# Layer B's sample result: turned in the bank `o` of the value product instead of the bank `tp` of the transposed queries and keys

## The chip, the cores and the metric

The kernel runs on one core of one Trainium2 chip. The metric is device time in microseconds (us) of one execution; lower is better. Engines are named as in the profile: PE is TensorE's matmul, PEld its weight load, DVE is VectorE, ACT is ScalarE, POOL is GpSimd, SP is the engine whose queue issues the DMAs.

## The reference, cut to what matters

Two layers of gated attention over a prompt of 2048 tokens and a "sample" of 64 new tokens with a cache. The second layer (B) has 16 heads of 64, a band of the own chunk of 64 and 8 chunks before it, and a bias by clipped distance:

```
q, k, v, gate = split(rms_norm(x) @ w_in)        # q and k normed per head
s = q @ k.T / 8 + bias(q_pos - k_pos)            # band for the prompt, cache + own for the sample
o = softmax(s) @ v
y = x + (o * silu(gate)) @ w_out
```

The sample goes through the same formula with 256 cached keys and its own 64.

## The kernel before

**Tiling.** Layer B goes through its 16 heads in eight passes of two heads each (`hp` = 0 to 7). In each pass the prompt is cut into units of 256 tokens (two tiles of 128), and the 64 sample tokens are a unit of their own. The order in a pass is prompt units 0 to 6, then the sample, then prompt unit 7. All products are float32 data in two float32r parts (a high and a low one).

**Order.** TensorE's order is written out by hand. Between the small steps of attention (scores, transposes of the weights, value products) a "filler" puts matmuls of the next input projection (lines 477 to 479, PSUM tile `pj`), and in the last pass those of the output projection (lines 1366 to 1368). The other engines' order is left to the tile scheduler, which follows its own estimate of times; semaphores between the engines come from the tiles that instructions share.

**Steps for a prompt unit.** `queries` (line 1072) transposes normed queries and keys into the PSUM tile `tp` (four transposes `tp<-ident,pa`); ACT takes the high parts out of it (lines 1095 and 1096), DVE the low parts (line 1100 for queries, line 1104 for keys, into `KA` and `KB`). The low parts are queued as background work. `scores` writes tile `sb` (lines 1146 and 1147); DVE adds the bias and takes the extreme (line 1150); ACT does the exponential (line 1154). `values` transposes the weights into `sb` (five `sb<-ident,p`), ACT and DVE split them into `ph` and `pl` (lines 581 and 582). `outputs` multiplies with the values into tile `o` (lines 1242 and 1243). On the second head it also transposes the gate tile `G` into `tp`. `G` is made on POOL (line 1168) out of reciprocals that DVE takes at line 1160.

**Steps for the sample.** `sample_outputs` multiplies weights and values into `o` (lines 1205 and 1206), ACT and DVE add the halves into an SBUF tile `o1` (lines 1209 and 1211), POOL multiplies with the gate (line 1212). Some steps later `sample_turned` (line 1214) transposes this tile once, and ACT writes the two halves out of PSUM, with the factor 0.5, into another `o1` tile (line 1219), which SP stores (line 1220).

**PSUM.** `tp` and `o` are tiles of one bank with one buffer each (`psum("tp", 512, 1)`, `psum("o", 512, 1)`), `pj` has two buffers, and `sb` has two of two banks each. A new tile in a pool of one buffer waits until every reader of the tile before it has finished.

**Place of the sample's steps.** While unit 7 is at work, the steps come in this order on PE: `values` of the sample, `values` of unit 7's first tile with `sample_outputs`, then `queries` of the next pass's unit 0 (which takes `tp`), a `scores`, another `values`, and then `sample_turned`. So in passes 0 to 6 the last tile in `tp` before the sample's transpose is that of the next pass's queries and keys. In pass 7 there is no next pass.

Of the kernel before, what the change touches and what calls it, by code (L numbers as in the profile page):

```python
# [50 lines left out]
def hybrid_encoder_kernel(  # L51
# [43 lines left out]
    def t(tag, shape, bufs=2, dt=F32):  # L95
        uid[0] += 1
        return sb.tile(shape, dt, tag=tag, name=f"{tag}_{uid[0]}", bufs=bufs)

    def psum(tag, cols, bufs, pool=None):
        uid[0] += 1  # L100
        return (pool or pp).tile([P, cols], F32, tag=tag, name=f"{tag}_{uid[0]}", bufs=bufs)
# [505 lines left out]
    def transpose(out, in_):  # L607
        n = in_.shape[0]
        nc.tensor.transpose(out, in_, ident[:n, :n])  # L609
# [396 lines left out]
    def layer_b():  # L1006
# [187 lines left out]
        def then(it, i, h):  # L1194
            if it.unit[0] == NU:
                return [lambda: sample_outputs(it), lambda: sample_turned(it)]
            if i == len(it.unit[2]) - 1:
                return [lambda: outputs(it, h)]
            return []
# [12 lines left out]
            nc.gpsimd.tensor_tensor(o, it.G[:, 0:HD], o, op=ALU.mult)  # L1212

        def sample_turned(it):
            tp = psum("tp", 512, 1)
            transpose(tp[0:HD, 0:P], it.o)
            o = t("o1", [P, 256])[:, 0:TS]
            for hh, r in enumerate(halves):
                nc.scalar.activation(o[r], tp[0:HD, hh * TS : (hh + 1) * TS], AF.Identity, scale=0.5)
            store(og[1][:, it.hp, SEQ:TOK], o)  # L1220
            finished[1, NU] = finished.get((1, NU), 0) + 1
# [290 lines left out]
```

## Time and profile before

| | us |
|---|---|
| median of 3 runs | 2322.2 (2320.93 to 2326.36) |
| the profiled execution, its time | 2330.51 |
| its span, first to last instruction | 2328.7 |
| PE busy | 2259.3 |
| DVE, ACT, POOL busy | 1559.2, 1432.8, 839.5 |
| mean granted TensorE clock, share of full speed | 0.991 |

All starts below are us from the start of the profiled span. A row of the timeline reads: start, duration, engine, line, operation, output tile <- input tiles, shapes, count, and in brackets the idle time of this engine just before, with the instruction that ended it. Layer B's attention runs from about 880 to 2170; what stands before is layer A, and behind it the rest of the output projection.

### The profile page before, as it was taken

The page shows a single profiled execution, that of the slowest core. Times are in us where ns is not written, and L with a number is a line of the kernel's source. Part 1 is how long each engine was busy: PE and PEld are TensorE (multiplying, and loading weights), DVE is VectorE, ACT ScalarE, POOL GpSimd, SP SyncE. Part 2 cuts the span into 40 slices and gives each one's busy share as a digit, 9 for nine tenths or more (in the row PEclk, how much of TensorE's full clock was granted, in tenths as well). Part 3 has the DMA queues.
Part 4 walks back from the last instruction along what each step waited for, and adds up shares of the span by engine and source line. Part 5 has one row for each costly group of instructions (what it writes and reads, how often), then busy time and mean ns, then how long its engine had stood idle before and what let it go on. Part 6 is the DMA issues. An engine that isn't in the chain of part 4 may idle for free.

```text
span 2328.7 us, 42202 instructions
## 1 busy us (share of the span) xinstructions
PE 2259.3 (97%) x13869; PEld 1984.3 (85%) x13869; DVE 1559.2 (67%) x5194; ACT 1432.8 (62%) x3632; POOL 839.5 (36%) x1196
## 2 busy tenths in 40 slices
PE   7899999999999999999999999999999999999999
PEld 6787888888889998888888888888888888888999
DVE  6779888887784446776767757667667577576211
ACT  6778877777773336765656656656556566565321
POOL 5554533333354556432222222222223222224443
PEclk9999999999999999999999999999999999999999
DMA  8846546754437767454543544544445435443665
GB/s 250 265 152 204 170 147 189 220 176 159 141 110 208 226 212 261 157 184 125 167 126 104 175 133 129 154 134 119 139 134 158 125 113 174 123 125 106 187 186 148
DMA packets 232124, 379.35 MB, mean 163 GB/s; under 512 B 24720, under 2 KB 163360, under 8 KB 231872
## 3 DMA queue, kind: packets, MB, share of 16 engines
q1 hardware_dynamic: 231904, 376.65, 52.7%
q8 instruction: 109, 1.79, 0.3%
q14 instruction: 111, 0.91, 0.1%
HBM read 296.13 MB, written 82.08 MB: 162 GB/s over the span
## 4 chain that ended last, share of the span: by engine, by line
PE 79%; DVE 8%; DMA 5%; ACT 4%; issue 2%; POOL 1%; SPq 1%; DVEq 0%; ACTq 0%; POOLq 0%
PE pj L477 13%; PE pj L479 12%; PE pj L478 12%; PE pj L1366 5%; PE pj L1367 5%; PE pj L1368 5%; PE sb L609 5%; PE o L1243 3%; PE o L1242 3%; PE tp L609 3%; PE sb L1147 3%; PE sb L1146 3%; DMA xraw<-in_x_rows_dram 2%; PE sa L609 2%; DVE pl L582 1%
## 5 line engine op out<-in xcount | busy, mean ns | idle before, releaser
L477 PE MATMUL pj<-wh,xx 128*128 128x512 f32 (+1 forms) x1648 | 671.0, 407 | 9.2 <-ACT pb L500 8.6
L479 PE MATMUL pj<-wh,xx 128*128 128x512 f32 (+1 forms) x1648 | 641.3, 389 | 0.0
L478 PE MATMUL pj<-wl,xx 128*128 128x512 f32 (+1 forms) x1648 | 638.7, 388 | 1.0 <-DVE wl L312 1.0
L479 PEld LDWEIGHTS pj<-wh,xx 128*128 128x128 f32 x1648 | 312.6, 190 | 68.3
L477 PEld LDWEIGHTS pj<-wh,xx 128*128 128x128 f32 x1648 | 314.1, 191 | 50.3 <-ACT pb L500 9.9
L478 PEld LDWEIGHTS pj<-wl,xx 128*128 128x128 f32 x1648 | 314.8, 191 | 40.0 <-DVE wl L312 1.4
L383 POOL TENSOR_TENSOR xx<-xraw,xx 128x528 fp32r<-128x528 f32 (+1 forms) x200 | 264.9, 1341 | 197.1 <-ACT xx L382 185.0
L540 POOL TENSOR_TENSOR f<-f,mhalf 128x4 f32<-128x4 f32 (+3 forms) x221 | 226.1, 1024 | 227.9 <-DVE f L536 219.0
L1154 ACT ACTIVATE p<-p,nm 128x640 f32<-128x640 f32 (+5 forms) x264 | 199.8, 757 | 175.2 <-DVE nm L1150 174.6
L1366 PE MATMUL pj<-xx,wh 128*128 128x264 f32 x1024 | 294.2, 287 | 1.2 <-DVE res L1371 1.0
L1367 PE MATMUL pj<-xx,wh 128*128 128x264 f32 x1024 | 291.7, 285 | 0.0
L1368 PE MATMUL pj<-xx,wl 128*128 128x264 f32 x1024 | 290.3, 283 | 0.0
L1150 DVE CUSTOM_DVE_ANT_0 p<-sb,BT 128x640 f32<-128x640 f32 (+5 forms) x272 | 196.8, 724 | 136.0 <-PE sb L1147 120.9
L582 DVE TENSOR_TENSOR pl<-sb,ph 128x640 fp32r<-128x640 f32 (+4 forms) x264 | 193.3, 732 | 117.0 <-ACT ph L581 114.2
L1002 POOL TENSOR_TENSOR o<-gt,o 128x256 f32<-128x256 f32 (+1 forms) x132 | 102.9, 779 | 386.1 <-DVE o L1001 122.8
L382 ACT CAST xx<-xraw 128x528 fp32r<-128x528 f32 (+1 forms) x200 | 122.2, 626 | 190.1 <-PE pj L1368 97.5
L581 ACT CAST ph<-sb 128x640 fp32r<-128x640 f32 (+4 forms) x264 | 163.5, 619 | 116.4 <-PE sb L609 111.1
L1366 PEld LDWEIGHTS pj<-xx,wh 128*128 128x128 f32 x1024 | 193.1, 189 | 2.1 <-DVE res L1371 1.6
L1367 PEld LDWEIGHTS pj<-xx,wh 128*128 128x128 f32 x1024 | 192.9, 188 | 0.2
L1368 PEld LDWEIGHTS pj<-xx,wl 128*128 128x128 f32 x1024 | 193.1, 189 | 0.0
L536 DVE CUSTOM_DVE_ANT_0 sq<-pa 128x64 f32<-128x64 f32 (+1 forms) x834 | 169.6, 256 | 30.8 <-ACT pa L500 28.8
L1371 DVE TENSOR_TENSOR res<-pj,res 128x264 f32<-128x264 f32 x128 | 55.0, 430 | 200.2 <-PE pj L1368 184.9
(210 smaller groups left out, 4788.6 us busy)
## 6 DMA issues: line engine op xcount, KB each, us to landing
xx<-xsb SPq DMA_DIRECT2D x224, 512.0 KB, 4.3
xx<-xsa SPq DMA_DIRECT2D x88, 512.0 KB, 4.8
xraw<-oga SPq DMA_DIRECT2D x64, 264.0 KB, 3.6
xraw<-ogb SPq DMA_DIRECT2D x64, 264.0 KB, 3.3
xsa<-xx SPq DMA_DIRECT2D x32, 512.0 KB, 4.5
wraw<-in_w_in_b_dram SPq DMA_DIRECT2D x64, 256.0 KB, 3.7
xsb<-xx SPq DMA_DIRECT2D x32, 512.0 KB, 4.0
xraw<-in_x_dram SPq DMA_DIRECT2D x40, 256.0 KB, 4.1
```

Of the source, the lines that this page charges most:

```text
L383: nc.gpsimd.tensor_tensor(xl, rv, xh.bitcast(F32), op=ALU.subtract)
L477: nc.tensor.matmul(ps[:n, :C], xh, wh, start=k == 0, stop=False)
L478: nc.tensor.matmul(ps[:n, :C], xh, wl, start=False, stop=False)
L479: nc.tensor.matmul(ps[:n, :C], xl, wh, start=False, stop=k == KC - 1)
L540: nc.gpsimd.tensor_tensor(fv, fv, mhalf[:n, :H], op=ALU.pow)
L582: b = nc.vector.tensor_tensor(dst_lo, src, dst_hi.bitcast(F32), op=ALU.subtract)
L609: nc.tensor.transpose(out, in_, ident[:n, :n])
L1150: mi = nc.vector.tensor_tensor_reduce(out=p[r, :nk], in0=S[r, o : o + nk], in1=b, op0=ALU.add, op1=ALU.min, scale=1.0, scalar=3e38, accum_ ...
L1154: ex = nc.scalar.activation(p[:n, :nk], p[:n, :nk], AF.Exp, scale=-1.0, bias=it.nm[:n, c : c + 1], accum_out=it.sm[:n, c : c + 1],)
L1366: nc.tensor.matmul(ps[:, :OT], wh, oh, start=k == 0, stop=False)
L1367: nc.tensor.matmul(ps[:, :OT], wh, ol, start=False, stop=False)
L1368: nc.tensor.matmul(ps[:, :OT], wl, oh, start=False, stop=k == KC - 1)
```

## The change

The PSUM tile of the sample's transpose is taken from the pool `o` instead of `tp`. Nothing else is edited.

```
         def sample_turned(it):
-            tp = psum("tp", 512, 1)
+            tp = psum("o", 512, 1)
             transpose(tp[0:HD, 0:P], it.o)
             o = t("o1", [P, 256])[:, 0:TS]
             for hh, r in enumerate(halves):
                 nc.scalar.activation(o[r], tp[0:HD, hh * TS : (hh + 1) * TS], AF.Identity, scale=0.5)
             store(og[1][:, it.hp, SEQ:TOK], o)
```

No instruction is added or removed, and the order on PE and SP stays. On PE the waits change. At the sample's transpose of pass 1 the order before is this (the engine names in brackets are the semaphores that an instruction waits for; numbers behind names are buffers, and the `o` on the right of the arrow is the SBUF tile `o1`):

```order
L609 MATMUL sb_15652<-ident,p_15560 128x128 x4
L609 MATMUL tp_15666<-ident,o_3141_15590 64x128 [waits DVE_49,PE_49,Pool_49]
L477 MATMUL pj_15645<-wh_14670,xx_15439 128x512 [waits DMAHW4_49]
L478 MATMUL pj_15645<-wl_14671,xx_15439 128x512
L1146 MATMUL sb_15678<-KB,q_3109_15424 128x384 [waits PE_49]
```

and now:

```order
L609 MATMUL sb_15652<-ident,p_15560 128x128 x4
L609 MATMUL o_15666<-ident,o_3141_15590 64x128 [waits PE_49,Activation_49,Pool_49]
L477 MATMUL pj_15645<-wh_14670,xx_15439 128x512 [waits DMAHW4_49]
L478 MATMUL pj_15645<-wl_14671,xx_15439 128x512
L1146 MATMUL sb_15678<-KB,q_3109_15424 128x384 [waits DVE_49]
```

(The five remaining filler matmuls between the last two rows are not shown.) The transpose waited for DVE's last reading of `tp` (line 1104, into `KB`); now it waits for ACT's reading of `o` (line 1209) and, through POOL's product (line 1212), for DVE's (line 1211). The next scores now carry a DVE wait of their own, for line 1150 of the scores before, which had been covered by the earlier wait.

The scheduler orders a few neighbours on the other engines differently. On ACT, in passes 1 to 6, behind the reading of the sample's transpose (pass 1 shown; `ph` is the high part of the weights, `p` the exponential):

```order
 L553 ACTIVATE sq_15663<-pb_15445 128x128
-L1219 ACTIVATE o_3158_15668<-tp_15666 64x64 x2
+L1219 ACTIVATE o_3158_15668<-o_15666 64x64 x2
+L581 CAST ph_15696<-sb_15698 128x5x128
 L1154 ACTIVATE p_15679,sm_15482<-p_15679,nm_15483 128x640
-L581 CAST ph_15696<-sb_15698 128x5x128
 L500 ACTIVATE pa_15725<-pj_15645,rms_93 128x384
```

The split of the weights now stands ahead of the exponential of the scores that follow; on DVE the low part (line 582) likewise moves ahead of the reciprocal (line 1160). On POOL, in passes 1 to 5, the gate product and the filling of a corner of the bias tile `BT`, which waits for a DMA (line 188), change places:

```order
 L561 TENSOR_TENSOR VT<-pa_15602,VT 128x2x64
+L189 MEMSET BT 64x64
 L1168 TENSOR_TENSOR G_15687<-pb_14989,sm_15482 128x128 x2
-L189 MEMSET BT 64x64
 L540 TENSOR_TENSOR f_15743<-f_15743,mhalf 128x4
```

So `G` of unit 7 now stands behind a step that waits for the bias DMA.

More of the change, by code (lines that the diff above doesn't have):

```diff
@@ L1214, in sample_turned @@
         def sample_turned(it):
-            tp = psum("tp", 512, 1)
+            tp = psum("o", 512, 1)
             transpose(tp[0:HD, 0:P], it.o)
```

## The prediction

> **What bounds the kernel now.** I read the page's busy times and chain first, then PE's waits in total, then the timeline around the longest of them.
>
> ```profile
> PE 2259.3 (97%) x13869; PEld 1984.3 (85%) x13869; DVE 1559.2 (67%) x5194; ACT 1432.8 (62%) x3632; POOL 839.5 (36%) x1196
> PE 79%; DVE 8%; DMA 5%; ACT 4%; issue 2%; POOL 1%; SPq 1%; DVEq 0%; ACTq 0%; POOLq 0%
> ...
> PE tp L609 <- DVE KB L1104: 21.7, 7, 3.4
> PE pj L477 <- ACT pb L500: 8.6, 5, 3.2
> ```
>
> PE is busy for 97% of the span and makes 79% of the chain that ended last, so the time is PE's busy time and its idle time. The largest entry in PE's waits (us in total, times, longest) is 21.7 us in seven pieces: a transpose into `tp` that waits for DVE's line 1104. The timeline shows that it is the sample's transpose in passes 0 to 6. Pass 1, on PE:
>
> ```profile
> 1195.17 0.71 PE L609 MATMUL sb<-ident,p 128*128 128x128 f32 x5
> 1199.23 0.40 PE L609 MATMUL tp<-ident,o 128*64 128x128 f32 x1 [3.34 <-DVE KB L1104]
> 1199.27 0.78 PE L477 MATMUL pj<-wh,xx 128*128 128x512 f32 x1
> 1199.85 0.63 PE L478 MATMUL pj<-wl,xx 128*128 128x512 f32 x1
> ...
> 1205.22 0.71 PE L609 MATMUL sb<-ident,p 128*128 128x128 f32 x5
> 1205.69 0.36 PE L1242 MATMUL o<-ph,VT 128*128 128x256 f32 x1
> ...
> 1210.16 0.71 PE L609 MATMUL sb<-ident,p 128*128 128x128 f32 x5
> ...
> 1213.81 0.38 PE L609 MATMUL tp<-ident,G 128*128 128x128 f32 x2
> ```
>
> The idle 3.34 us are not all. The matmuls behind it start 0.42 us apart and last 0.63 us; in pass 0, where the same transpose waits only half as long, they start 0.23 us apart and last 0.39 us:
>
> ```profile
> 1038.15 0.71 PE L609 MATMUL sb<-ident,p 128*128 128x128 f32 x5
> 1040.56 0.27 PE L609 MATMUL tp<-ident,o 128*64 128x128 f32 x1 [1.70 <-DVE KB L1104]
> 1040.90 0.39 PE L478 MATMUL pj<-wl,xx 128*128 128x512 f32 x1
> 1041.13 0.40 PE L479 MATMUL pj<-wh,xx 128*128 128x512 f32 x1
> ...
> 1044.05 0.71 PE L609 MATMUL sb<-ident,p 128*128 128x128 f32 x5
> ...
> 2155.93 0.71 PE L609 MATMUL sb<-ident,p 128*128 128x128 f32 x5
> 2156.48 0.27 PE L609 MATMUL tp<-ident,o 128*64 128x128 f32 x1
> ```
>
> The last two rows are pass 7, which has no queries of a next pass in `tp`: the transpose follows without a wait, 0.55 us after the five before it. A table of stretches, each from one five-fold transpose to the next (pass 0 to pass 6), gives the length, the busy times of PE, PEld, DVE, ACT and POOL, and then the granted clock:
>
> ```profile
> 1038.15:1044.05 5.90, 4.20 (x23) 3.41 (x22) 4.22 (x13) 3.33 (x9) 0.46 (x1) 1.00 0.69 204
> 1195.17:1205.22 10.05, 6.71 (x23) 5.39 (x22) 5.25 (x16) 3.56 (x10) 1.53 (x2) 0.66 0.20 66
> 1355.10:1365.37 10.27, 6.94 (x23) 5.57 (x22) 5.29 (x16) 3.54 (x10) 1.56 (x3) 0.67 0.20 69
> 1515.15:1524.04 8.89, 5.54 (x24) 4.45 (x23) 5.14 (x15) 2.95 (x9) 1.54 (x2) 0.81 0.19 71
> 1674.00:1683.09 9.09, 5.75 (x24) 4.64 (x23) 5.27 (x16) 3.55 (x10) 1.53 (x2) 0.81 0.21 71
> 1832.95:1843.24 10.29, 6.94 (x24) 5.57 (x23) 5.32 (x16) 3.56 (x10) 1.56 (x3) 0.67 0.20 68
> 1993.19:2001.99 8.80, 5.47 (x23) 4.39 (x22) 5.11 (x15) 2.93 (x9) 1.53 (x2) 0.81 0.20 71
> sum 63.29, PE 41.54 PEld 33.42 DVE 35.60 ACT 23.41 POOL 9.71; mean PE 5.93 PEld 4.77 DVE 5.09 ACT 3.34 POOL 1.39
> ```
>
> The instructions are the same in each stretch. Pass 0 kept the clock at 1.00 and passes 1 to 6 had 0.66 to 0.81. So an idle of 1.70 us leaves the clock alone here, and one of 3.34 us takes it down for a time that varies.
>
> **The change part by part.** *The wait that goes.* A stretch without wait and at full clock is 0.55 us (pass 7, from the five-fold transpose to the sample's) plus 1044.05 - 1040.56 = 3.49 us (pass 0, from there to the next five-fold one) = 4.04 us. Seven of them are 28.28 us, and the table's sum is 63.29 us. The difference is 35.0 us. Its parts: 1.86 us in pass 0 and 4.76 to 6.25 us in each of the others. What the slow clock makes of it is the time from the sample's transpose to the next five-fold one beyond 3.49 us; in pass 1 that is 1205.22 - 1199.23 - 3.49 = 2.50 us, and the shortest and longest stretch give 1.3 and 2.7 us. Over six passes it comes to about 12 us, and idle time to about 23 us.
>
> [...]
>
> *The wait that comes.* The transpose now needs the bank `o` and the finished product. In pass 1 these are done here (DVE's last reading of `o`, POOL's product), and the rows below them carry the next steps:
>
> ```profile
> 1192.73 0.45 DVE L1211 TENSOR_TENSOR o<-o,o 64x64 f32<-64x64 f32 x2
> 1193.72 0.33 POOL L1212 TENSOR_TENSOR o<-G,o 128x64 f32<-128x64 f32 x1
> ...
> 1197.25 0.82 DVE L582 TENSOR_TENSOR pl<-sb,ph 128x640 fp32r<-128x640 f32 x1
> 1198.59 0.49 DVE L1104 SCALAR_TENSOR_TENSOR KB<-tp,ksc,KB 64x256 fp32r<-64x256 f32 x1
> 1199.31 0.29 DVE L554 SCALAR_TENSOR_TENSOR pb<-sq,pb 128x128 f32<-128x128 f32 x1
> 1203.29 0.82 DVE L1150 CUSTOM_DVE_ANT_0 p<-sb,BT 128x640 f32<-128x640 f32 x1 [3.68 <-PE sb L1147]
> ...
> 1197.11 0.31 ACT L553 ACTIVATE sq<-pb 128x128 f32<-128x128 f32 x1
> 1199.66 0.45 ACT L1219 ACTIVATE o<-tp 64x64 f32<-64x64 f32 x2 [2.23 <-PE tp L609]
> ...
> 1204.15 0.33 SPq L188 DMA_DIRECT2D BT<-skew x1
> 1205.43 0.76 POOL L1168 TENSOR_TENSOR G<-pb,sm 128x128 f32<-128x128 f32 x2 [8.42 <-DVE sm L1160]
> ```
>
> POOL ends at 1194.05 and PE arrives at 1195.17 + 0.55 = 1195.72, so 1.67 us are to spare: cost 0.
>
> *What is late next.* With PE 6.0 us earlier, the next five-fold transpose comes at 1195.17 + 4.04 = 1199.21. It needs the buffer of `sb` that DVE's line 582 leaves at 1198.07; 1.1 us to spare, the narrowest place of this pass. DVE still has lines 1104 and 554 to do until 1199.60; then line 1150 for the scores in between, which PE has ready before that, until 1200.42. PE needs its bank again at about 1202.5 (1208.55 in the trace, less 6.01) and its weights, through ACT's exponential, at 1210.16 - 6.01 = 1204.15. DVE's low splits are no longer in PE's way; the 3.68 us that DVE idles at line 1150 are what it catches up in.
>
> *The bank `o`.* The next value product (1205.69 - 6.01 = 1199.68) must wait for ACT's line 1219. ACT is free for it at 1197.42 and needs 0.45 us, so 1197.87: 1.8 us to spare.
>
> *The exchanged neighbours.* ACT's split of the weights starts when the transposes end (1199.21 + 0.71 = 1199.92) and, at about 0.7 us, ends near 1200.6; the exponential could have started at about 1200.5. It loses 0.1 us of the 3.6 us that it has: cost 0. The bias DMA on SP follows line 1150 by 1204.15 - 1203.29 = 0.86 us, so it is issued at about 1200.5; from issue to landing the bias loads take:
>
> ```profile
> DMA to landing us min/median/max: 1.9/2.9/7.0
> ```
>
> At the median POOL's fill is done near 1203.5 and `G` near 1204.3, against the transposes of `G` at 1213.81 - 6.01 = 1207.80: 3.5 us to spare. At 7.0 us `G` would be 0.6 us late, five times 0.6 = 3 us at worst. I take 0.
>
> In pass 7 the transpose had no wait and gets none: 0.
>
> **The sum.** The profiled execution would go from 2330.5 to 2330.5 - 35.0 = 2295.5 us. The runs shown have a median of 2322.2, 8.3 us below the profiled one; the stalls are of the same program, so I take the same 35.0 us off: 2287.2 us, 1.5% faster. The clock's part can differ from run to run: with 1.3 or 2.7 us in all six passes the gain is 31 or 39 us, and the time 2291 or 2283.
>
> **The rivals.**
>
> *A second wait takes the place (2297).* DVE's line 582 or a later one holds the next five-fold transpose. For: only 1.1 us to spare, and DVE works off its queue without a rest until 1199.60. Against: nothing ahead of line 582 on DVE, ACT or POOL waits for what the change moves. Pass 0 shows that a rest of 1.7 us does not touch the clock, so at six times 1.7 us the gain falls by 10 us to 25.
>
> *The clock falls nevertheless (2299).* The slow phase would have another reason than the idle time, and only the idle 23 us go. For: all six begin in the same place. Against: pass 0, with the same instructions and a shorter idle, stays at 1.00. [...]
>
> *No change (2322).* The new wait ends as late as the old. That needs `o` or POOL's product 3.4 us later than they are shown; POOL's row ended 1.67 us ahead of need in pass 1.
>
> *Slower (over 2327).* The bias DMA, now ahead of `G` on POOL, comes so late that PE waits for `G` longer than it gained. Five passes have the exchange; to lose 35 us and 5 more, each must wait 8 us, so the load must land 3.5 + 2.9 + 8 = 14 us after issue. The longest here took 7.0.
>
> **How the numbers follow.** The forecast, 35 us give or take the clock's part, gets 0.77 and the range 2283 to 2292; the second wait 0.13; the clock that falls anyway 0.05; no change 0.03; slower 0.02. For 8 in 10 the range takes in the forecast and the second wait, and a little below the largest gain: 2281 to 2298. A difference under 0.2% (4.6 us) cannot be told from none here; all cases but the last two are faster by more, so faster 0.95, the same 0.03, slower 0.02.
>
> **What the profile after would show.** The entry of `tp` behind line 1104 is gone from PE's waits; the sample's transpose, now `o<-ident,o`, starts about 0.55 us after the five-fold one; the seven stretches are about 4.0 us long with a granted clock of 1.00, and the mean clock is near 1.00 instead of 0.991. DVE's line 1150 behind it starts at once after line 554. Wrong would be: a new bracket of over 1 us at line 609 (`sb`) naming line 582, at line 1242 naming line 1219, or at the transposes of `G` naming POOL; or stretches at a lower clock with no idle time ahead of them.

## The result, and the profile after

| | before | after |
|---|---|---|
| median of the runs beside each other, us | 2322.5 (2320.9 to 2326.4, 4 runs) | 2294.5 (2290.4 to 2295.8, 4 runs) |
| ratio after to before, 95% interval | | 0.9874 [0.9857, 0.9892] |
| repeated (experiment e5), us | 2326.7 (2321.2 to 2333.8, 9 runs) | 2294.4 (2292.2 to 2296.2, 5 runs) |
| ratio, 95% interval | | 0.9857 [0.9836, 0.9877] |
| profiled execution, span | 2330.5, 2328.7 | 2295.8, 2294.0 |
| mean granted clock | 0.991 | 0.996 |

The change made the kernel 1.3 to 1.4% faster. Between the two profiled executions the difference is 34.7 us, between the medians first shown 28.0, and between those of the repetition 32.3. Why these differ is the main question left; e1 and e3 answer a part of it.

The longest of PE's waits in the profile after (us in total, times, longest):

```profile
PE o L947 <- DVE pl L582: 6.4, 8, 1.5
PE o L477 <- ACT wh L309: 6.3, 1, 6.3
PE pj L477 <- ACT pb L500: 5.9, 4, 3.8
PE sb L609 <- DVE pl L582: 4.9, 8, 1.2
```

The entry `PE tp L609 <- DVE KB L1104` with its 21.7 us is gone. Of the others, the wait behind ACT's line 500 is 2.7 us shorter than before (5.9 against 8.6), but it was 3.2 us in another profile of the kernel before (e1), so it varies by itself; the rest were there before in about the same size. Pass 1 on PE, and then what DVE, ACT, SP and POOL do there:

```profile
1193.97 0.71 PE L609 MATMUL sb<-ident,p 128*128 128x128 f32 x5
1194.51 0.27 PE L609 MATMUL o<-ident,o 128*64 128x128 f32 x1
1194.54 0.47 PE L477 MATMUL pj<-wh,xx 128*128 128x512 f32 x1
...
1197.98 0.71 PE L609 MATMUL sb<-ident,p 128*128 128x128 f32 x5
1198.44 0.36 PE L1242 MATMUL o<-ph,VT 128*128 128x256 f32 x1
...
1206.57 0.38 PE L609 MATMUL tp<-ident,G 128*128 128x128 f32 x2
```

```profile
1196.04 0.82 DVE L582 TENSOR_TENSOR pl<-sb,ph 128x640 fp32r<-128x640 f32 x1
1197.41 0.49 DVE L1104 SCALAR_TENSOR_TENSOR KB<-tp,ksc,KB 64x256 fp32r<-64x256 f32 x1
1198.13 0.29 DVE L554 SCALAR_TENSOR_TENSOR pb<-sq,pb 128x128 f32<-128x128 f32 x1
1198.45 0.82 DVE L1150 CUSTOM_DVE_ANT_0 p<-sb,BT 128x640 f32<-128x640 f32 x1
...
1196.12 0.43 ACT L1219 ACTIVATE o<-o 64x64 f32<-64x64 f32 x2
...
1199.31 0.33 SPq L188 DMA_DIRECT2D BT<-skew x1
...
1201.46 0.14 POOL L189 MEMSET BT<- 64x64 f32 x1 [5.64 <-DMA BT<-skew]
1201.57 0.76 POOL L1168 TENSOR_TENSOR G<-pb,sm 128x128 f32<-128x128 f32 x2
```

The sample's transpose follows 0.54 us after the five before it, while DVE's line 1104 ends only at 1197.90. The work that PE waited for is still as late as it was; PE no longer needs it here. DVE goes from line 554 straight into line 1150, where it had idled 3.68 us. The seven stretches between the five-fold transposes (length; busy PE, PEld, DVE, ACT, POOL; clock; the last two columns are the DMA's share and rate):

```profile
1038.84:1042.87 4.03, 4.03 (x23) 3.46 (x22) 3.94 (x11) 3.04 (x9) 0.46 (x1) 1.00 0.87 282
1193.97:1197.98 4.01, 4.01 (x23) 3.44 (x22) 3.87 (x12) 2.52 (x8) 1.55 (x2) 1.00 0.37 130
...
1963.61:1967.62 4.01, 4.01 (x23) 3.44 (x22) 3.87 (x12) 2.50 (x8) 1.54 (x2) 1.00 0.40 137
sum 28.12, PE 28.12 PEld 24.14 DVE 27.20 ACT 18.12 POOL 9.71; mean PE 4.02 PEld 3.45 DVE 3.89 ACT 2.59 POOL 1.39
```

Their sum is 28.12 us against 63.29: 35.2 us less, and PE is busy for all of it at the full clock. So the profiled pair's 34.7 us stand in these seven places, to half a microsecond.

### The profile page after: what moved, and what is told of

Its sections match the earlier page's. It is cut to its first block, busy times and chain, and to the rows that moved or that the text cites. A ratio compares the mean times of both kernels' runs of the same rounds, so it can differ in the third digit from the quotient of the medians.

```text
span 2294.0 us, 42216 instructions
## 1 busy us (share of the span) xinstructions
PE 2250.2 (98%) x13869; PEld 1978.8 (86%) x13869; DVE 1559.1 (68%) x5194; ACT 1431.2 (62%) x3632; POOL 838.8 (37%) x1196
## 4 chain that ended last, share of the span: by engine, by line
PE 60%; DVE 4%; ACT 2%; issue 1%; DMA 1%; POOL 1%; SPq 0%; POOLq 0%; ACTq 0%; DVEq 0%
PE pj L477 9%; PE pj L479 9%; PE pj L478 9%; PE sb L609 5%; PE pj L1366 5%; PE pj L1367 5%; PE pj L1368 5%; PE o L1243 3%; PE o L1242 3%; PE sb L1147 3%; PE sb L1146 3%; PE tp L609 2%; ACT p L1154 1%; DVE pl L582 1%; DVE p L1150 1%
```

## The experiments

Theory A: the change takes away one wait of PE, which costs a fixed idle time and, behind it, a slow clock that differs from execution to execution. The rivals doubt the clock's part, its cause, or that the bank alone does it.

**e1: the kernel before, unchanged.** No edit.

> The kernel before, unchanged, to see how its executions differ. The profiled execution of before took 2330.5 us, its other runs 2320.9 to 2326.4; after takes 2290.4 to 2295.8. Theory A (the idle time is fixed, the slow clock behind it is not, and the profiled execution of before had more of it than most): runs between 2320 and 2331, the longer ones at the lower granted clock (0.991 at 2330, about 0.993 to 0.995 at 2321), idle at the sample's transpose 21.7 us in every profile. Rival B (the clock's share is the same in all, and the profiled execution was long for another reason, layer A or the profiler): the clock is 0.991 in all runs and the stretches at the seven transposes sum to 63.3 us again.

Measured: 2325.3 us median over 11 runs (2321.8 to 2330.0), and 2326.9 over 17 more runs of before that stood beside e1 to e4. With e5's nine there are 37 runs of before, with a median of 2326.35 us. By the granted clock of each run:

```
granted clock   runs   mean us
0.994              2    2321.9
0.993              6    2324.8
0.992             19    2326.2
0.991              5    2327.9
0.990              2    2327.6
0.989              3    2332.8
```

The waits on line 1104 in the new profile, and its stretches (first, longest, sum):

```profile
PE tp L609 <- DVE KB L1104: 21.7, 7, 3.4
```

```profile
1036.16:1042.05 5.89, 4.19 (x24) 3.40 (x23) 4.23 (x13) 3.33 (x9) 0.47 (x1) 1.00 0.64 204
...
1669.74:1679.99 10.25, 6.92 (x24) 5.55 (x23) 5.30 (x16) 3.54 (x10) 1.53 (x3) 0.67 0.17 56
...
sum 61.01, PE 39.27 PEld 31.64 DVE 35.60 ACT 23.45 POOL 9.66; mean PE 5.61 PEld 4.52 DVE 5.09 ACT 3.35 POOL 1.38
```

The idle time is the same to a tenth; the sum of the stretches is 2.3 us shorter than in the first profile, all of it slow clock (only one of six passes has 0.67, where three had 0.66 or 0.67). Theory A holds, rival B (the same clock in every run) does not. Of the first four runs of before three took 2322.75 us or less, and of these 37 only three did: the median that the prediction started from lay at the low end, and why is not shown.

**e2: the bank stays `tp`, six filler matmuls ahead of the transpose.**

```
-                    if nxt is not None:
+                    late = x > 0 and its[x - 1].unit[0] == NU and y == 2
+                    if nxt is not None and not late:
                         nxt()
...
                     goal(2 * y + 2)
+                    if late:
+                        nxt()
```

> The bank stays tp, but the transpose of the sample stands behind the six filler matmuls (1.4 us) that followed it. The wait on line 1104 falls from 3.34 to about 1.9 us in passes 1 to 6 and from 1.70 to about 0.3 in pass 0: 10 us less idle. Theory A (idle above some length takes the clock down; 1.70 us did not): the clock stays up, so the clock's share goes as well: 5 us in usual runs, 12 in one like the profiled execution of before; gain 15, 2307 us, granted clock 0.996 or more. Rival B (the clock falls at this place whatever the idle): gain 10, 2312 us, stretches still at 0.66 to 0.8.

Measured: 2311.4 us, ratio 0.9939 [0.9925, 0.9952] to before, 15.4 us less than the 2326.9 beside it. The waits, and the stretches of passes 1 to 6:

```profile
PE tp L609 <- DVE KB L1104: 12.1, 7, 2.0
```

```profile
1191.76:1197.98 6.22, 4.18 (x24) 3.29 (x23) 5.21 (x17) 2.96 (x9) 1.54 (x2) 1.00 0.33 110
1347.93:1355.42 7.49, 5.55 (x23) 4.28 (x22) 5.30 (x16) 3.55 (x10) 1.71 (x3) 0.80 0.27 88
1505.53:1511.67 6.14, 4.18 (x23) 3.30 (x22) 5.13 (x15) 2.95 (x9) 1.54 (x2) 1.00 0.26 91
1661.63:1668.85 7.22, 5.27 (x24) 4.01 (x22) 5.30 (x16) 3.55 (x10) 1.67 (x3) 0.83 0.29 96
1819.21:1826.91 7.70, 5.73 (x23) 4.49 (x22) 5.32 (x16) 3.56 (x10) 1.71 (x3) 0.78 0.26 88
1976.83:1982.95 6.12, 4.18 (x24) 3.29 (x22) 5.12 (x15) 2.94 (x9) 1.54 (x2) 1.00 0.28 97
```

The idle time fell by 21.7 - 12.1 = 9.6 us as said. The clock did not do what either theory said: with 1.94 to 2.04 us of idle it fell in three passes of six. The total of 15.4 us came out as forecast, but for another reason: the clock's share of usual runs is larger than the 5 us that I put in (9.2 us, e3), and 15.4 - 9.6 = 5.8 us of it went.

The length of the wait does not say which passes fall: the longest, 2.04 us in pass 1, kept the clock. Its place does. The three slow phases of these passes (3.41 us at a granted clock of 0.50) begin at 1352.43, 1666.46 and 1823.47, that is 92 and 46 times 3.4133 us apart, so one can lay a grid of such steps over the span. The step with the wait and the step behind it, in pass 2 and in pass 3:

```profile
1349.02:1352.43 3.41, 1.47 (x8) 0.97 (x7) 3.27 (x7) 1.27 (x5) 0.75 (x2) 1.00 0.14 51
1352.43:1355.84 3.41, 3.41 (x11) 2.72 (x11) 1.01 (x3) 1.21 (x4) 0.59 (x2) 0.50 0.19 48
1506.03:1509.44 3.41, 1.60 (x8) 0.98 (x6) 3.34 (x8) 1.72 (x4) 1.35 (x2) 1.00 0.29 102
1509.44:1512.86 3.42, 3.27 (x22) 3.00 (x23) 1.51 (x5) 1.79 (x5) 0.23 (x1) 1.00 0.17 39
```

Length less busy PE, the step with 1.94 us of idle was followed by a slow step, and the one with 1.81 us was not. In passes 4 and 5, where the clock fell, the step had 1.95 and 1.97 us; in passes 1 and 6, where it stayed up, the edge of a step cuts the wait and leaves 1.56 and 1.55 us in the larger part.

**e3: the bank stays `tp`, and matmuls fill the wait.** Their product is read by nobody.

```
         def sample_turned(it):
+            if 1 <= it.hp <= 6:
+                fill = psum("o", 512, 1)
+                for _ in range(14):
+                    nc.tensor.matmul(fill, VT[:, 8, 0], KA[:, 1024:1536], start=True, stop=True)
             tp = psum("tp", 512, 1)
```

> The bank stays tp and the order stays, but in passes 1 to 6 fourteen matmuls of 512 columns, whose result nobody reads, fill the wait (14 x 0.233 = 3.26 us) into the free bank o. Theory A: PE is busy while it waits, the clock does not fall, and the time is before less the clock's share alone: about 5 us less in usual runs (2317), up to 12. Rival B (the clock's fall does not come from the idle): no change, 2322, clock still down behind the transpose. If it is slower than 2322, the added matmuls delay something that I do not see.

Measured: 2317.7 us (2312.8 to 2319.9), ratio 0.9959 [0.9944, 0.9974], 9.2 us less than before although PE has 84 matmuls more. Pass 2 on PE, and its stretch:

```profile
1352.39 0.71 PE L609 MATMUL sb<-ident,p 128*128 128x128 f32 x5
1352.85 3.46 PE L1218 MATMUL o<-KA,VT 128*128 128x512 f32 x14
1356.43 0.27 PE L609 MATMUL tp<-ident,o 128*64 128x128 f32 x1
```

```profile
1352.39:1359.91 7.52, 7.40 (x38) 5.92 (x37) 5.12 (x15) 2.95 (x9) 1.54 (x2) 1.00 0.21 76
```

PE is as late as before at the transpose, but it works while it waits; the clock stays at 1.00 in all six stretches (0.66 to 0.81 in the profile of before), and the clock's share alone is won. This shows that the idle time takes the clock down, and prices the clock's share in usual runs at 9.2 us (6 to 13 by the interval). The stretch of 7.52 us is 3.51 us longer than after's 4.01; six of these and pass 0's 1.86 us make 22.9 us of idle. 22.9 + 9.2 = 32.1 us, and e5 measured 32.3.

**e4: the change in passes 1, 3 and 5 alone.**

```
-            tp = psum("tp", 512, 1)
+            tp = psum("o" if it.hp in (1, 3, 5) else "tp", 512, 1)
```

> The change in passes 1, 3 and 5 alone; the others keep tp. Theory A and B both: what is won is won pass by pass: three of the six passes with the long wait, so about half of the 26 us that passes 1 to 6 bring, 13 us: 2309 us, and three long waits and one short one are left (11.7 us in the waits on line 1104). Rival C (the gain comes from one place, or is given back later in the span): the gain is far from 13, say under 6 or over 20.

Measured: 2310.5 us, ratio 0.9932 [0.9919, 0.9945]: 16.3 us less. Half of the 32.3 us less pass 0's 1.86 is 15.2, so the gain is made pass by pass (rival C is out); the 13 us expected were half of a gain that itself was taken too small. The waits that are left on line 1104 are 11.7 us, as expected. The last changed and the last unchanged pass:

```profile
1821.21:1825.24 4.03, 4.03 (x24) 3.46 (x22) 3.89 (x12) 2.53 (x8) 1.54 (x2) 1.00 0.44 150
1975.28:1982.80 7.52, 4.19 (x24) 3.41 (x23) 5.11 (x15) 2.94 (x9) 1.52 (x2) 1.00 0.24 82
```

The second row, pass 6, has the full wait (3.33 us by the timeline) and yet a clock of 1.00. The slow phases of this profile in passes 2 and 4 begin at 1353.02 and 1667.05; on the grid of 3.4133 us through them, the wait of pass 2 lies mostly in one step, and that of pass 6 is cut in the middle:

```profile
1349.61:1353.02 3.41, 0.67 (x6) 0.44 (x4) 3.31 (x11) 2.16 (x6) 1.53 (x2) 1.00 0.40 147
1353.02:1356.43 3.41, 2.81 (x8) 2.26 (x9) 0.95 (x3) 0.43 (x2) 0.00 (x0) 0.50 0.04 10
1974.25:1977.66 3.41, 1.73 (x11) 1.22 (x9) 3.33 (x15) 3.20 (x8) 1.96 (x4) 1.00 0.66 224
1977.66:1981.07 3.41, 1.76 (x9) 1.52 (x10) 1.97 (x5) 0.43 (x2) 0.00 (x0) 1.00 0.07 21
```

Pass 2 has 2.74 us of idle in one step, pass 6 has 1.68 and 1.65 us in two.

**e5: the changed kernel again.** No edit against after.

> The changed kernel once more, beside fresh runs of before. Seventeen further runs of before had a median of 2326.9 us, above the four that stood beside the result (2322.5). Theory A (the idle of 23 us is fixed, the clock's share of before varies and is about 9 us in usual runs, as the filled wait showed): after stays at 2294 to 2296, before at 2325 to 2328, so the gain is 31 to 33 us, ratio 0.986 to 0.987. Rival B (the 28 us of the first result is the true gain and 35 us of the profiled pair an accident): the ratio is 0.988 or more.

Measured: 2294.35 us (2292.2 to 2296.2) beside 2326.69 for before; ratio 0.9857 [0.9836, 0.9877], gain 32.3 us. Theory A's numbers hold; the interval reaches to 0.9877, so 28 us is just outside it.

**e6: the bank stays `tp`, twelve filler matmuls and the scores ahead of the transpose.**

```
                     goal(2 * y + 1)
+                    if later is not None:
+                        later()
+                        later = None
                     nxt = todo.pop(0) if todo else None
...
+                    if x > 0 and its[x - 1].unit[0] == NU and y == 2:
+                        nxt, later = None, nxt
```

> The bank stays tp, and the sample's transpose stands behind twelve filler matmuls and the scores between them (3.4 us of PE's work), so that line 1104 is done when PE comes to it. Theory A (all that the change does is to take this wait away, and the exchanged neighbours on ACT, DVE and POOL cost and bring nothing): as after, 2294 to 2297. Rival B (part of the gain comes from the other order on ACT, DVE and POOL): 5 us or more behind after. Rival C (the wait moves on: in tp the transpose now stands closer to the next use of tp): new waits at line 609 (tp) of over 0.5 us per pass.

Measured: 2294.6 us (2293.6 to 2299.6, 4 runs), ratio 0.9863 [0.9841, 0.9885]: the same as after. The transpose has no wait in any pass; pass 2:

```profile
1350.41 0.27 PE L609 MATMUL tp<-ident,o 128*64 128x128 f32 x1
1350.53 0.74 PE L609 MATMUL sb<-ident,p 128*128 128x128 f32 x5
```

So the bank as such and the exchange on POOL, which has the old order here, are worth nothing that can be measured (0.3 us between the medians, with runs 6 us apart): a way that keeps the bank and only gives DVE time does the same. Rival C falls, there is no new wait at `tp`. Rival B falls for POOL alone, because ACT and DVE have the order of the changed kernel in e6 too (line 581 ahead of 1154, line 582 ahead of 1160); for these two it is the sum under e3 that leaves nothing over, 32.1 of 32.3 us.

**e7: the changed kernel, and in pass 7 more filler before unit 7's first scores.**

```
                     goal(2 * y + 2)
+                    if sample and x + 2 == len(its):
+                        filler.to(filler.done + 2.0)
```

> The changed kernel, and in pass 7 alone 2.0 us more filler matmuls between the transposes of unit 7's queries and its first scores. There after still has two waits on DVE's low parts (line 1108 0.44 us, line 1100 1.37 us) and a clock of 0.57 to 0.75 behind them for about 4 us. Theory A (a wait that PE can fill with work that it has to do anyway is won, clock and all): 1.8 us of idle and 1 to 2 us of the clock less, 2291 to 2292 against 2294.5; at the edge of what can be measured, so the waits in the profile decide. Rival B: what is filled in there is missing later and the time is the same.

Measured: 2290.4 us (2288.0 to 2294.5, 4 runs), ratio to before 0.9842 [0.982, 0.9864]. The scores, first in e5's profile of after and then here:

```profile
2105.78 0.44 PE L1146 MATMUL sb<-KA,q 128*128 128x384 f32 x1 [0.44 <-DVE q L1108]
2107.60 0.44 PE L1147 MATMUL sb<-KA,q 128*128 128x384 f32 x1 [1.38 <-DVE q L1100]
```

```profile
2105.93 0.34 PE L1146 MATMUL sb<-KA,q 128*128 128x384 f32 x1
2106.10 0.33 PE L1147 MATMUL sb<-KA,q 128*128 128x384 f32 x1
```

The waits are gone, and the median is 3.9 us below e5's beside it. The runs of both overlap, so that it beats after is likely and not shown. The same two waits had 3.41 us at a clock of 0.50 behind them in the first profile of after (from 2107.86) and none in e5's.

## Why the prediction was right, and by how much it was off

The forecast was 2287.2 us (2281 to 2298), faster; measured were 2294.5 and 2294.4.

- *The wait that goes.* Right, and to size: 35.0 us forecast for the profiled execution, 34.7 measured, 35.2 in the stretches themselves.
- *The wait that comes, and what is late next.* Right place by place. Line 582 ends 1.1 us before the five-fold transpose (1196.86 and 1197.98; forecast 1.1). ACT's line 1219 ends at 1196.55, 1.9 us before line 1242 (forecast 1.8). `G` is ready at 1202.33, 4.2 us before its transposes (forecast 3.5; the bias load took about 2.2 us). None of the waits that I named as signs of error appeared.
- *The clock.* The mechanism was right (e3), the rule of thumb too simple. "An idle of 1.70 us leaves the clock alone here, and one of 3.34 us takes it down" held in the one profile that I had. e2 and e4 show that the length of the wait does not decide: waits of 2.04 us (e2, pass 1) and 3.33 us (e4, pass 6) kept the clock, and one of 1.94 us (e2, pass 2) did not. What went with the falls there was how much idle time lay in one step of 3.41 us, and that differed from execution to execution. And the "time that varies" had two values: in before the phases were 3.41 or 6.83 us long, and a fall cost less than half of that where PE still waited in a part of it (pass 6: slow from 1996.64, the wait until 1997.22, 1.3 us lost).
- *The sum, against the median.* Here the step failed, in its size. "I take the same 35.0 us off" used the clock's share of one profiled execution, 12 us, which was a long one: 2330.5 us, where 37 runs have a median of 2326.35. In usual runs the share is 9.2 us (e3), so the gain is 32 us. And it was taken off 2322.2, the median of three runs, 4.1 us below that of the 37. The two errors add up: 4.1 + 2.7 = 6.8 of the 7.2 us between forecast and result. The 8.3 us between profiled execution and median, which the prediction noted and set aside, were the sign of this.
- *The range.* That 2294.5 us lies inside it is partly luck. The forecast's own bounds were 2283 to 2292 us, with a chance of 0.77, and the result is above them; the range reached up to 2298 only to take in the second wait, which did not come.
- *The rivals.* A second wait did not come, the clock stayed up at the seven places, and the bias load was not late.

## What to carry to other kernels

The PSUM tile in a pool of one buffer made its next user wait here for the slowest reader of the one before (21.7 us in seven waits on line 1104), and that reader belonged to a step that has nothing to do with the one that waited; look at who read the bank last, and take a bank whose last reader has finished, or put work that has to be done anyway ahead of the step. Price an idle of PE as long as those here (3.3 us, with 1.3 to 2.7 us of slow clock behind it in before) with the matmuls behind it, from the same stretch without the wait and not from the bracket alone. And where the clock makes runs differ, do not subtract the loss of one profiled execution from a median of three others.

## What the runs showed of the hardware

- In the profiles of before and after the granted clock had two levels, 1.00 and 0.50. Behind the waits on line 1104 of before it was 0.50 for 6.83 us in passes 1, 2 and 5 (from 1197.92, 1358.35 and 1836.22) and for 3.41 us in passes 3, 4 and 6 (from 1518.77, 1679.20 and 1996.64). In order of time these six starts lie 47, 47, 47, 46 and 47 times 3.4133 us apart; two slow phases of after, from 227.11 and 2107.86, lie 551 times that apart.
- What went with a fall was how much idle time lay in one step of this grid. In the stretches of the sample's transposes (passes 0 to 6 of before, e3 and e4, passes 1 to 6 of e2) every step at full clock with 1.94 us or more of idle was followed by a slow one (11 of 11: six in before, three in e2, two in e4), and none with 1.81 us or less was, pass 0 of before with its wait of 1.70 us included. In e1 the six passes with the full wait fell too, with clocks of 0.67 and 0.81 in their stretches. None of the 11 steps was idle throughout; the most was 2.91 us (before, 1515.36 to 1518.77). Idle time alone does not settle it: in pass 7 a step with 1.54 us (e3; waits of 1.38 and 0.16 us) and one with 1.81 us (after, from 2104.44) were followed by slow ones, and in pass 3 of e2 one with 1.81 us was not.
- The grid lay differently under the same waits in the two profiled executions of before: pass 1 had 6.83 us of slow clock in the first and 3.41 us in e1's (clock of its stretch 0.66 and 0.81). The spread of the kernel before goes with the clock, from a mean of 2321.9 us at 0.994 to 2332.8 at 0.989, but not with it alone: at 0.993 the runs go from 2321.2 to 2327.9 us. After, with those six places gone, nine runs lie within 5.8 us.
